# Other starting bytes for the token rows that TensorE streams in a hybrid decoder layer

## The chip, the cores and the metric

The kernel runs on one core of a Trainium2 chip. The metric is the device time of one execution in microseconds (us). Before the change it is 1539.64 us, the median of 3 runs (1539.16 to 1542.01). The execution that the profiler recorded took 1543.23 us; its span, from the first to the last instruction, is 1541.5 us.

## The reference

One layer of a decoder trunk: 4096 new tokens and 64 sample tokens, model width 1024. What matters here is the first of its steps, the projection of all 4160 tokens through one weight matrix of 1024 by 2816:

```python
h = _rmsnorm(x, g_pre)
z = h @ w_in
cb, cc, ch, cg, q, k, v, ag, mq, mg = _split_cols(z)
...
y = jnp.concatenate([out_a, out_b, out_c], axis=-1) @ w_out
return x + _rmsnorm(y, g_post), new_conv, new_k, new_v
```

Between the two products stand a gated short convolution, a sliding window attention with sinks, and a cross attention into 256 memory tokens. All of it is float32.

## The kernel before, in words

The kernel has two parts. The first, up to about 935 us, is the input projection; the second is the attention and the output projection (line 1501).

**How a float32 product is made.** TensorE is fed float32r operands. To keep float32 accuracy each operand is split into a rounded part `hi` and a remainder `lo`, and a product is three matmuls: weights hi times tokens hi, weights hi times tokens lo, weights lo times tokens hi. `product` (lines 370 to 376) does that for four slices of 128 contraction rows: 12 matmuls of 128x128 weights by 260 token columns into one PSUM bank. Line 375 is the matmul, with its weight load.

**How the projection is staged.** `w_in` has 22 column tiles of 128. They are done in three phases of 4, 4 and 3 pairs of tiles (`PHASES`, line 44). The tokens go in 8 blocks of 520, each two halves of 260 columns. A block with a pair of column tiles is a 2x2 by 2x2 block product with Strassen's scheme in Winograd's form, seven products instead of eight (`PRODUCTS`, line 41). Only the first two blocks of the first phase take the plain eight (`PLAIN_BLOCKS`, line 45, `plain_block`, line 676). So a step is one of the seven token operands (B11, B21, T2, T3, T1, B22, T4) used by the 4 or 3 pairs ("quads" in the code, loop at line 983): 48 matmuls of line 375 in the first two phases, 36 in the third. All in all there are 7488 of them: 2 blocks x 8 products x 4 x 12 = 768 plain ones, then 6 x 7 x 4 x 12 = 2016, 8 x 7 x 4 x 12 = 2688 and 8 x 7 x 3 x 12 = 2016.

**What sets the order.** The order of all engines' instructions in the projection is written out by hand (`tc.manual_schedule`, line 699). In each step the next step's token operand is split first (`h_split(i + 1)`, line 946): ScalarE casts x to `hi` (line 365) and VectorE subtracts to `lo` (line 366). Each instruction handles 128 x 1040 elements, four rows of 260 per partition. `x_split` (line 584) does the same row by row in the plain blocks. VectorE and ScalarE also add the finished banks into the z tiles (`evict`, line 378).

**Where the operands lie.** `hi` and `lo` come from the pool `hp`, two buffers each. A buffer holds per partition four rows of `XR` = 320 elements, 1280 bytes, of which 260 are used; `split_tile` (lines 357 to 361) says at which element the 260 begin, from the list `begins` (line 355), whose two entries are taken in turn, so that each of the two buffers keeps one of them. 1280 is five times 256, and the buffers begin at multiples of 256 bytes, so all four rows of a buffer have the same starting byte modulo 256. Before, these are:

| buffer pair | hi rows begin at, modulo 256 | lo rows begin at, modulo 256 |
|---|---|---|
| A | 32 | 160 |
| B | 64 | 192 |

Steps alternate between A and B. The weight slices of the first three quads (w_0, w_1, w_2 in the profile's names, pool `wa`) begin at 0 modulo 256, those of the fourth (w_3, pool `wb`, `w_slot` at line 173) at 224; a slice of 128 columns is 512 bytes.

Of the kernel before, what the change touches and what calls it, by code (L numbers as in the profile page):

```python
# [52 lines left out]
def hybrid_layer(ctx: ExitStack, tc: tile.TileContext, a: dict):  # L53
# [298 lines left out]
                tc.keep_in_program_order(ins)  # L352
            store(hd[b][o], ops[o])

    begins = {"hi": [8, 16], "lo": [40, 48]}

    def split_tile(tag, name):

# [1333 lines left out]
```

## Time and profile before

| what | value |
|---|---|
| median of 3 runs | 1539.64 us (1539.16 to 1542.01) |
| profiled execution | 1543.23 us, span 1541.5 us |
| granted TensorE clock, mean | 0.998 |
| input projection, line 375 | about 6 to 935 us |
| attention and output projection | about 935 to 1541 us |

Names such as `hi_5T` or `w_0S` are the program's tile names with buffer numbers left out: `hi_5T` is the rounded part of one of block 5's T operands, `w_0S` the weights of quad 0 for one of the S operands. PE is TensorE's matmuls, PEld its weight loads, DVE VectorE, ACT ScalarE, POOL GpSimd. A matmul's recorded duration runs past the start of the next one, since matmuls are pipelined; what a matmul costs is the distance from its start to the next start. In the chain of waits, "x36" after a piece says that 36 instructions in a row were on the chain.

### The profile page before, as it was taken

The numbers are of one execution on the slowest core, as the hardware profiler recorded it, in microseconds if no ns is written. First come the engines' busy times: TensorE is split into PE (matmuls) and PEld (weight loads), VectorE is DVE, ScalarE is ACT, GpSimd is POOL, SyncE is SP. The second block draws the span as 40 slices with busy tenths as digits, with TensorE's granted clock in tenths as the row PEclk, the third lists the DMA queues.
The fourth block names the chain that finished last, engine by engine and source line by source line (L and its number), as shares of the span: only waits on it lengthen the run. The fifth ranks groups of instructions, "written<-read, shape, count | busy, mean of one in ns | idle before, by whom it ended". The sixth has DMA issues, their size and how long they took to land.

```text
span 1541.5 us, 30150 instructions
## 1 busy us (share of the span) xinstructions
PE 1529.6 (99%) x11331; PEld 1407.2 (91%) x11331; DVE 1147.0 (74%) x2055; ACT 806.8 (52%) x2039; POOL 380.8 (25%) x604
## 2 busy tenths in 40 slices
PE   9999999999999999999999999999999999999998
PEld 9999999999999999999999998788888888888877
DVE  6779888898988777887787678766666666666643
ACT  6776566476222222354454447665566556555632
POOL 0223332211400000000101203544444444444310
PEclk9999999999999999999999999999999999999999
DMA  9989999778755333678777789976767676776433
GB/s 267 195 215 242 268 281 268 272 240 290 193 180 180 126 125 126 216 221 286 232 264 229 227 293 257 225 161 155 158 148 148 148 155 157 155 159 152 130 109 96
DMA packets 177942, 306.28 MB, mean 199 GB/s; under 512 B 33925, under 2 KB 107653, under 8 KB 177765
## 3 DMA queue, kind: packets, MB, share of 16 engines
q1 hardware_dynamic: 130901, 227.38, 47.5%
q0 software_dynamic: 46176, 75.92, 24.0%
q8 instruction: 90, 1.47, 0.4%
q10 hardware_dynamic: 720, 1.05, 0.2%
q14 instruction: 55, 0.45, 0.1%
HBM read 197.23 MB, written 108.05 MB: 198 GB/s over the span
## 4 chain that ended last, share of the span: by engine, by line
PE 93%; DVE 3%; DMA 2%; issue 1%; ACT 0%; POOL 0%; DVEq 0%; SPq 0%; POOLq 0%; ACTq 0%
PE c L375 55%; PE y L1501 22%; PE ws L1255 4%; PE wo L1097 2%; PE wt L1278 2%; PE xs L1191 2%; PE xt L1206 2%; PE wo L1227 2%; PE wo L1233 1%; PE mem_acc L798 1%; DMA qd<-z 1%; DVE z L382 0%; DMA wr_1A<-in_w_in 0%; DMA xr<-in_x_p 0%; DVE wo L186 0%
## 5 line engine op out<-in xcount | busy, mean ns | idle before, releaser
L1501 PE MATMUL y<-wo,mh 128*128 128x512 f32 (+1 forms) x1040 | 350.8, 400 | 0.0
L382 DVE TENSOR_TENSOR z<-c,z 128x520 f32<-128x520 f32 (+1 forms) x308 | 194.5, 644 | 94.3 <-PE c L375 92.5
L1501 PEld LDWEIGHTS y<-wo,mh 128*128 128x128 f32 x1040 | 194.5, 188 | 39.3 <-issue 2.4
L1501 PE MATMUL y<-wo,ml 128*128 128x512 f32 (+1 forms) x520 | 201.8, 388 | 0.0
L1268 ACT ACTIVATE sm<-sm,wnm 128x128 f32<-128x128 f32 x256 | 99.6, 391 | 60.8 <-DVE wnm L1262 59.3
L1200 POOL TENSOR_SCALAR xp<-xp,xrd 128x256 f32<-128x256 f32 x128 | 74.9, 593 | 209.2 <-DVE xrd L1196 209.2
L1501 PEld LDWEIGHTS y<-wo,ml 128*128 128x128 f32 x520 | 98.2, 189 | 16.5
L1192 DVE TENSOR_REDUCE xmx<-xs 128x2 f32<-128x512 f32 x64 | 44.1, 689 | 59.7 <-PE xs L1191 59.6
L1280 ACT COPY wpt<-wt 128x512 f32<-128x512 f32 x64 | 37.3, 583 | 88.9 <-PE wt L1278 86.4
L1255 PEld LDWEIGHTS ws<-kst,q 128*128 128x128 f32 x512 | 70.3, 191 | 5.6 <-ACT xp L1195 0.7
L1508 DVE TENSOR_TENSOR yn<-y,gpost 128x512 f32<-128x512 f32 (+1 forms) x66 | 45.0, 682 | 39.9 <-PE y L1501 39.6
L1255 PE MATMUL ws<-kst,q 128*128 128x256 f32 x512 | 73.7, 284 | 0.4 <-ACT xp L1195 0.4
L1509 ACT ACTIVATE y<-y 128x512 f32<-128x512 f32 (+1 forms) x66 | 38.6, 585 | 64.1 <-DVE yn L1508 64.1
L746 POOL CAST wmask<-negs 128x256 uint8<-128x256 f32 x1 | 1.0, 1037 | 267.2 <-DMA negs<-in_wmask 267.2
L1288 POOL TENSOR_SCALAR_AFFINE_SELECT wpt<-wpt 128x512 f32<-128x512 f32 x64 | 52.8, 825 | 42.2 <-ACT wpt L1280 39.2
L1195 ACT ACTIVATE xp<-xs,xnm 128x256 f32<-128x256 f32 x128 | 59.0, 465 | 7.1 <-DVE xnm L1193 7.1
L1130 POOL DMA_DIRECT2D q<-qd x64 | 42.9, 675 | 70.7 <-DVE wo L186 60.9
L1519 DVE SCALAR_TENSOR_TENSOR xr<-yn,yst,xr 128x1024 f32<-128x1024 f32 (+2 forms) x34 | 43.5, 1281 | 15.5 <-POOL yst L1515 13.4
L1119 POOL DMA_DIRECT2D kst<-qd x64 | 38.7, 617 | 63.8 <-PE xt L1206 41.5
L1258 DVE COPY_PREDICATED sm<-wmask,ws 128x256 f32<-128x256 uint8 x124 | 52.1, 436 | 2.5 <-ACT sm L1257 2.3
L1285 POOL TENSOR_SCALAR_AFFINE_SELECT wpv<-wpt 128x512 f32<-128x512 f32 x62 | 40.4, 652 | 52.1 <-ACT wpt L1280 52.0
L384 ACT COPY z<-c 128x520 f32<-128x520 f32 (+1 forms) x44 | 24.4, 554 | 52.9 <-PE c L375 50.0
(962 smaller groups left out, 5121.4 us busy)
## 6 DMA issues: line engine op xcount, KB each, us to landing
q<-qd POOLq DMA_DIRECT2D x64, 384.0 KB, 7.2
xr<-in_x_p SPq DMA_DIRECT2D x32, 512.0 KB
nat<-in_x_p SPq DMA_DIRECT2D x39, 416.0 KB
o_yp<-xr SPq DMA_DIRECT2D x31, 512.0 KB
md<-th POOLq DMA_DIRECT2D x48, 260.0 KB, 6.3
qd<-zh SPq DMA_DIRECT2D x48, 260.0 KB
qd<-z SPq DMA_DIRECT2D x48, 260.0 KB
kst<-qd POOLq DMA_DIRECT2D x60, 192.0 KB, 5.9
```

Of the source, the lines that this page charges most:

```text
L375: TE.matmul(bank[:, :HW], l, r, start=first and i == 0, stop=last and i == 3 * KH - 1)
L382: add = lambda dst, other: V.tensor_tensor(dst, c, other, op=ALU.add)
L1192: V.tensor_reduce(mx[:, :nb], s, axis=AX.X, op=ALU.max)
L1195: S.activation(p[:, i, :], s[:, i, :], AF.Exp, bias=nm[:, i : i + 1], scale=SCALE, accum_out=den[:, i : i + 1])
L1200: G.tensor_scalar(p[:, i, :], p[:, i, :], rd[:, i : i + 1], 0.5, op0=ALU.mult, op1=ALU.mult)
L1255: TE.matmul(s3[:, hh, :], self.q[:, 4 + 2 * (2 * half + hh) + kvh, i * P : i * P + P], self.kst[:, 2 * kvh + part, i * P : i * P + 2 * P], ...
L1258: V.copy_predicated(sm[:, 2 * half : 2 * half + 2, :], third["wmask"], third["negs"] if first else s3[:, :, 0:P])
L1268: S.activation(sm[:, hh, :], sm[:, hh, :], AF.Exp, bias=nm[:, hh : hh + 1], scale=SCALE, accum_out=den[:, hh : hh + 1])
L1288: G.affine_select(p3, p3, pattern=[[0, 4], [1, P]], compare_op=ALU.is_ge, fill=0.0, base=0, channel_multiplier=-1)
L1501: TE.matmul(acc, self.hl[l][:, k], wo[k][c0 // 512][:, r, c0 % 512 : c0 % 512 + c1 - c0], start=j == 0, stop=j == passes * KT - 1)
L1508: V.tensor_tensor(yn[:m, c0:c1], acc[:m], gpost[:m, c0:c1], op=ALU.mult)
L1519: V.scalar_tensor_tensor(self.xr[:m, cs], yn[:m, cs], st[:m, 3:4], self.xr[:m, cs], op0=ALU.mult, op1=ALU.add)
```

## The change

One line: the elements at which the 260 columns of a row begin. The rows of `hi` begin at 16 or 144 bytes modulo 256, those of `lo` at 80 or 208. In 16-byte units these are the odd numbers 1, 9, 5 and 13, where before they were the even ones 2, 4, 10 and 12. The weights stay at 0 and 224, which are even numbers of 16 bytes.

```diff
-    begins = {"hi": [8, 16], "lo": [40, 48]}
+    begins = {"hi": [4, 36], "lo": [20, 52]}
```

Tile sizes, addresses of buffers, instructions and their order stay as they are. The last row of a buffer now ends at element 52 + 260 = 312 of 320.

## Prediction

> **What bounds the kernel now.** I read the page first, then the chain of waits in order of time, then the timeline of two steps of the projection, then the stretches.
>
> ```profile
> span 1541.5 us, 30150 instructions
> PE 1529.6 (99%) x11331; PEld 1407.2 (91%) x11331; DVE 1147.0 (74%) x2055; ACT 806.8 (52%) x2039; POOL 380.8 (25%) x604
> ...
> PE 93%; DVE 3%; DMA 2%; issue 1%; ACT 0%; POOL 0%; DVEq 0%; SPq 0%; POOLq 0%; ACTq 0%
> PE c L375 55%; PE y L1501 22%; PE ws L1255 4%; PE wo L1097 2%; PE wt L1278 2%; PE xs L1191 2%; PE xt L1206 2%; PE wo L1227 2%; PE wo L1233 1%; PE mem_acc L798 1%; DMA qd<-z 1%; DVE z L382 0%; DMA wr_1A<-in_w_in 0%; DMA xr<-in_x_p 0%; DVE wo L186 0%
> ```
>
> TensorE is the chain for 93% of the span, and 55 points of that are line 375, the only line whose operands the change moves. The chain in order of time gives its pieces (start, length, count):
>
> ```profile
> 113.80 238.98 PE c L375 x1992
> 355.91 305.13 PE c L375 x2542
> ...
> 786.70 0.95 PE ws L1255 x8
> 787.65 4.24 PE c L375 x36
> 791.89 0.96 PE ws L1255 x8
> 792.85 4.32 PE c L375 x36
> ...
> 797.62 4.24 PE c L375 x36
> ...
> 802.30 4.33 PE c L375 x36
> ...
> 1007.23 2.78 PE y L1501 x12
> ```
>
> Two things are to be seen. In the first two phases matmuls follow one another without a wait: 238.98 / 1992 = 119.97 ns and 305.13 / 2542 = 120.04 ns. In the third, whole steps of 36 alternate between 4.32 to 4.33 us (120 ns each) and 4.24 us (117.8 ns each). Same shape, same count, same weight pool: only the buffer pair, so the starting bytes, and the moment differ. So the cost of a matmul does depend on something like the edited line.
>
> The timeline shows the same inside a step of 48. Here are the starts of the four quads of a step on pair A (240.36), of the next on pair B (246.10), and of the one after.
>
> ```profile
> 240.36 0.28 PE L375 MATMUL c<-hi_5T,w_0S 128*128 128x260 f32 x1
> ...
> 241.80 0.28 PE L375 MATMUL c<-hi_5T,w_1S 128*128 128x260 f32 x1
> ...
> 243.24 0.28 PE L375 MATMUL c<-hi_5T,w_2S 128*128 128x260 f32 x1
> ...
> 244.68 0.28 PE L375 MATMUL c<-hi_5T,w_3S 128*128 128x260 f32 x1
> ...
> 246.10 0.28 PE L375 MATMUL c<-hi_5T,w_0S 128*128 128x260 f32 x1
> ...
> 247.53 0.28 PE L375 MATMUL c<-hi_5T,w_1S 128*128 128x260 f32 x1
> ...
> 248.97 0.28 PE L375 MATMUL c<-hi_5T,w_2S 128*128 128x260 f32 x1
> ...
> 250.41 0.28 PE L375 MATMUL c<-hi_5T,w_3S 128*128 128x260 f32 x1
> ...
> 251.25 0.29 PE L375 MATMUL c<-lo_5T,w_3S 128*128 128x260 f32 x1
> 251.38 0.41 PE L375 MATMUL c<-hi_5T,w_3S 128*128 128x260 f32 x2
> ...
> 251.87 0.28 PE L375 MATMUL c<-hi_5B,w_0S 128*128 128x260 f32 x1
> ```
>
> Twelve matmuls of a quad take 1.44, 1.44, 1.44 and 1.42 us on pair A, and 1.43, 1.44, 1.44 and 1.46 us on pair B. The fourth quad has its weights at 224 instead of 0 modulo 256: with them pair A is cheaper (118.3 ns) and pair B dearer (121.7 ns). With the weights at 0 both pairs cost 120 ns here, though pair B costs 117.8 in the third phase. So a price depends on rows and weights together, and one pair of addresses can have two.
>
> What meets there is visible in the weight loads of the same stretch:
>
> ```profile
> 240.12 0.19 PEld L375 LDWEIGHTS c<-hi_5T,w_3S 128*128 128x128 f32 x1
> 240.24 0.19 PEld L375 LDWEIGHTS c<-hi_5T,w_0S 128*128 128x128 f32 x1
> 240.36 0.19 PEld L375 LDWEIGHTS c<-lo_5T,w_0S 128*128 128x128 f32 x1
> ```
>
> Every matmul has its own load, and the load for the next starts when the matmul starts (both 240.36): while 260 columns stream, 128 columns of weights are read from the same memory.
>
> **The change, part by part.** It adds and removes no instruction, no wait and no transfer, and moves none past a queue. Three kinds of instruction touch the moved rows.
>
> The matmuls of line 375: 7488 by the loops, 2 x 8 x 48 plain, then 6 x 7 x 48, 8 x 7 x 48 and 8 x 7 x 36. All lie on the path (the pieces above hold no wait), so 1 ns each is 7.5 us. No row shows float32r rows at an odd multiple of 16 bytes, so I bound the price. Cheapest of the rows: 4.24 / 36 = 117.8 ns. Dearest: 1.46 / 12 = 121.7 ns over a quad, and one spacing of 0.13 us between two starts (251.25 to 251.38) inside it. A floor below that comes from other shapes. Eight matmuls of 256 columns take 0.95 us, 119 ns each; twelve of 512 take 2.78 us, 231.7 ns each. So a column costs (231.7 - 119) / 256 = 0.44 ns, 260 of them 114.5 ns, and about 5.5 ns is there whatever the width (an estimate from these rows); that is what could go if it is a collision of the two reads and the new places remove it.
>
> I take 120 ns, no change. It is the price that three of four quads pay now on both pairs, although the pairs stand differently to the weights: 32 and 160 against 64 and 192. A price that stayed when rows moved by 32 bytes is the likeliest after a move by 16. The fourth quad pays 118.3 and 121.7, on average 120 again. Term: 7488 x 0 = 0 us.
>
> [...]
>
> The two splits, ScalarE's cast to `hi` and VectorE's subtraction to `lo`, write rows that begin elsewhere (and VectorE reads `hi` there):
>
> ```profile
> L365 ACT CAST hi_5T<-x_5T 128x1040 fp32r<-128x1040 f32 x8 | 8.5, 1066 | 13.4 <-PE c L375 9.7 <-issue 3.7
> L366 DVE TENSOR_TENSOR lo_5T<-x_5T,hi_5T 128x1040 fp32r<-128x1040 f32 x8 | 9.9, 1239 | 1.2 <-ACT hi_5T L365 1.2
> ...
>   DVE lo_0B L366: 0.8, 2
>   DVE lo_0T L366: 0.5, 2
>   DVE lo_2T L366: 0.5, 2
> ```
>
> The last three rows are of line 375's own waits: with all 7488 matmuls, TensorE waited for `lo` 1.8 us. A split takes 1.07 + 1.24 = 2.3 us and is made one step ahead, in a step of 5.74 us, so 3.4 us of cover hide even a doubling of it; a cheaper split gives at most those 1.8 us. Bound on this term: -1.8 to about +2 us, taken as 0. Without that cover each nanosecond of the pair would count once in each of some 160 steps. Between these, other engines have little room to matter:
>
> ```profile
> 50.00:340.00 290.00, 289.89 (x2412) 289.44 (x2411) 242.90 (x312) 185.41 (x334) 77.90 (x125) 1.00 0.92 250
> 340.00:550.00 210.00, 209.84 (x1750) 209.44 (x1749) 176.75 (x241) 76.20 (x107) 24.68 (x28) 1.00 0.57 185
> ```
>
> The columns are length, then busy time of PE, PEld, DVE, ACT and POOL, granted clock, share of the DMA engines, GB/s. In the first phase the DMA engines are 92% busy and VectorE 84%: up to some 8% of TensorE's time could go before they become the bound. No case below asks for more than 5%.
>
> The sum: the profiled execution has 1541.5 us of span and 1.7 us around it (1543.23 in all); 0 + 0 leaves that. The runs shown have a median of 1539.64, 3.6 us below the profiled one, so I forecast 1539.6 us in the terms of the median. A measurement of this kernel can tell about 0.2%, 3.1 us, from no change; that is 0.41 ns of a matmul.
>
> **The rivals.**
>
> *The cheap price everywhere.* Pair B's third-phase steps show that a regular stream at 117.8 ns exists with the weights at 0. If the new places lead to it from any moment, the plain blocks and first two phases (5472 matmuls) save 120.0 - 117.8 = 2.2 ns each, 12.0 us, and half of the third phase's 56 steps save 0.09 us each, 2.5 us: 1541.5 falls by 14.5, the median to 1525. For it: rows and weights now all begin at even multiples of 16 bytes, so an odd start separates them in a way not seen yet. Against it: pair B reaches that price in the third phase and not in the second with the same addresses, so the moment decides as well.
>
> *The collision goes.* If the 5.5 ns are gone, 7488 x 5.5 = 41 us, 1498. TensorE's time falls under 5%, which the 92% of the DMA engines still allow. For it: the constant is there. Against it: it is there at all shapes and places that the rows show, none of which comes below 117.8.
>
> *The dear price everywhere (slower).* On pair B with weights at 224 the quads run at 121.7 ns. If rows at an odd multiple of 16 bytes meet the weights as badly, with weights at 0 too, it is (121.7 - 120) x 7488 = 13 us: 1552. It decides from the point at which a quad of twelve with w_0 passes 1.445 us (120.4 ns). For it: such a quad exists in each step on pair B. Against it: it is one place out of four.
>
> *Worse than any quad seen.* If each matmul took the single spacing of 0.13 us, rounded; its neighbours being 0.12, I put it at 125 ns: 5 x 7488 = 37 us, 1577. Against it: no twelve in a row do so.
>
> **How the numbers follow.** No change 0.31, the cheap price 0.28, no collision 0.09, the dear price 0.25, worse 0.07. I rank no change first since the same 120 ns holds on two different pairs, but not by much: the fourth quad shows that moves of this size shift a price by 2 ns either way. Faster by over 0.2%: 0.28 + 0.09 = 0.37; within 0.2%: 0.31; slower: 0.25 + 0.07 = 0.32. The forecast's own range is 1536.5 to 1542.7. The range for 8 times in 10 takes in the cheap and the dear price with the splits' bounds and some of what lies beyond: 1518 to 1556; left out are most of 0.09 and 0.07.
>
> **What would show it.** The piece of 1992 matmuls in the chain: 239 us if I am right, 234.6 at the cheap price, 242.4 at the dear one, 228 without collision. The quads of a step in the timeline: 1.44 us, against 1.41, 1.46 and 1.37. The third phase's steps of 36: still a mixture of 4.24 and 4.33 us if moment and place decide together; one length alone if the place decides. The cast and the subtraction should stay at 1.07 and 1.24 us, and lines 1501 and 1255 at their prices, since their operands lie elsewhere. I am wrong if the spacing of matmuls with w_0 leaves 120 ns by more than 0.4, or if line 375 starts to wait for `hi` or `lo`.

## The result and the profile after

The change makes the kernel slower by a third of a per cent.

| | median | lowest to highest | profiled execution | its span |
|---|---|---|---|---|
| before | 1540.07 us | 1539.06 to 1542.01 | 1543.23 us | 1541.5 us |
| after | 1545.24 us | 1544.15 to 1548.24 | 1547.25 us | 1545.5 us |

The ratio of the times is 1.0035, with a 95% interval of 1.0024 to 1.0046: 5.2 us, between 3.7 and 7.1. All engines carry out the same instructions in the same order. The page after begins:

```profile
span 1545.5 us, 30150 instructions
...
PE 1533.0 (99%) x11331; PEld 1410.5 (91%) x11331; DVE 1146.0 (74%) x2055; ACT 806.6 (52%) x2039; POOL 380.5 (25%) x604
```

The busy time of TensorE's matmuls rose by 3.4 us, that of its weight loads by 3.3, and no other engine's rose. The chain of waits in order of time (start, length, count) has the pieces that were 238.98 us for 1992 matmuls, 305.13 us for 2542, and 4.24 or 4.33 us for a step of the third phase:

```profile
114.30 240.66 PE c L375 x1992
...
486.50 205.67 PE c L375 x1703
...
788.06 4.34 PE c L375 x36
...
793.35 4.32 PE c L375 x36
...
798.62 4.32 PE c L375 x36
...
803.38 4.33 PE c L375 x36
```

240.66 / 1992 and 205.67 / 1703 are both 120.8 ns, where it was 120.0. In the third phase the steps of 4.24 us are gone: those without a wait now take 4.31 to 4.36 us, about 120 to 121 ns a matmul, on both buffer pairs.

The timeline shows one step on pair A (hi at 16, lo at 80) and the next on pair B (144, 208). The starts of their quads are:

```profile
241.66 0.29 PE L375 MATMUL c<-hi_5T,w_0S 128*128 128x260 f32 x1
...
243.12 0.28 PE L375 MATMUL c<-hi_5T,w_1S 128*128 128x260 f32 x1
...
244.57 0.28 PE L375 MATMUL c<-hi_5T,w_2S 128*128 128x260 f32 x1
...
246.02 0.28 PE L375 MATMUL c<-hi_5T,w_3S 128*128 128x260 f32 x1
...
247.49 0.28 PE L375 MATMUL c<-hi_5T,w_0S 128*128 128x260 f32 x1
...
253.25 0.29 PE L375 MATMUL c<-hi_5B,w_0S 128*128 128x260 f32 x1
```

Pair A's quads take 1.46, 1.45, 1.45 and 1.47 us, its step 5.83 us or 121.5 ns a matmul; pair B's step takes 253.25 - 247.49 = 5.76 us, 120.0 ns. Before, the two steps took 5.74 and 5.77 us. Only pair A became dearer in this stretch.

Pair A doesn't pay that price all the time. TensorE waits for `lo` just before 358.1 us (0.15 us) and again just before 444.8 us (0.21 us), and between these two waits pair A's steps take as long as pair B's. Here are the starts of one of them and of the step behind it:

```profile
392.52 0.28 PE L375 MATMUL c<-hi_1B,w_0A 128*128 128x260 f32 x1
...
398.29 0.28 PE L375 MATMUL c<-hi_1T,w_0S 128*128 128x260 f32 x1
```

That is 5.77 us, 120 ns a matmul. For some 230 us before the first of these waits and again after the second, pair A's steps take 5.83 us, 121.4 ns, with the same starting bytes. So even within the first two phases the moment takes part: each of these changes came with a wait.

From here on "spacing" is the mean distance between the starts of one matmul of line 375 and the next, over the whole trace, with the distances of 150 ns and more (waits) left out. It was 119.73 ns and is 120.40 ns, and it rose in each phase: from 119.87 to 120.49, from 119.81 to 120.48 and from 119.41 to 120.17 ns. The mean difference, 0.68 ns before rounding, times 7488 is 5.1 us: nearly all of the measured 5.2 us.

Two smaller things changed. Line 375's own waits for `lo`, 1.8 us before, are now these:

```profile
  DVE lo_3T L366: 1.9, 2
...
  DVE lo_2T L366: 0.9, 3
...
  DVE lo_0T L366: 0.5, 2
  DVE lo_0B L366: 0.3, 1
```

That is 3.6 us, 1.8 more. (The view counts the idle time of a weight load and of its matmul one by one, so a wait stands in it twice.) And the last matmul of line 375 starts 6.4 us later (941.07 us after the span's start, 934.69 before), 0.5 us of which the first already had. The span grew by 4.0 us only, so the second part of the kernel gave 2.4 us back, 1.4 of them in the first long wait of the chain there. In the chain before it is

```profile
942.87 10.70 DMA qd<-z
```

and in the chain after

```profile
949.17 9.35 DMA qd<-z
```

### The profile page after: what moved, and what is told of

It is laid out like the page before. It is cut to its first block, busy times and chain, and to the rows that moved or that the text cites. A ratio compares the mean times of both kernels' runs of the same rounds, so it can differ in the third digit from the quotient of the medians.

```text
span 1545.5 us, 30150 instructions
## 1 busy us (share of the span) xinstructions
PE 1533.0 (99%) x11331; PEld 1410.5 (91%) x11331; DVE 1146.0 (74%) x2055; ACT 806.6 (52%) x2039; POOL 380.5 (25%) x604
## 3 DMA queue, kind: packets, MB, share of 16 engines
q8 instruction: 90, 1.47, 0.4%
## 4 chain that ended last, share of the span: by engine, by line
PE 92%; DVE 4%; DMA 2%; issue 1%; ACT 1%; SPq 0%; POOL 0%; DVEq 0%; POOLq 0%; ACTq 0%
PE c L375 53%; PE y L1501 22%; PE ws L1255 4%; PE wo L1097 2%; PE wt L1278 2%; PE xs L1191 2%; PE xt L1206 2%; PE wo L1227 2%; PE wo L1233 1%; PE mem_acc L798 1%; DMA qd<-z 1%; DVE z L382 0%; DMA xr<-in_x_p 0%; DMA ws20A<-in_w_in 0%; DVE wo L186 0%
```

## The experiments

The theory is that the time goes with line 375's spacing and that the spacing is set by where the moved rows stand to the weights. The rivals: that odd multiples of 16 bytes are bad as such; that the place modulo 64 decides, or the distance between `hi` and `lo`; that only one of the two rows matters; and that the moment decides. All edits are given against the kernel after, but for half_before; ratios are to the kernel before, run beside it.

### Other places of the same rows: rows_0, rows_32, rows_48, odd_128

```diff
-    begins = {"hi": [4, 36], "lo": [20, 52]}
+    begins = {"hi": [0, 32], "lo": [16, 48]}     # rows_0
+    begins = {"hi": [8, 40], "lo": [24, 56]}     # rows_32
+    begins = {"hi": [12, 44], "lo": [28, 60]}    # rows_48
+    begins = {"hi": [4, 20], "lo": [36, 52]}     # odd_128
```

The first three move all rows of the change by the same 16 bytes or a multiple, so that hi and lo stay 64 bytes apart; odd_128 uses the change's own four bytes but pairs them 16 with 144 and 80 with 208.

rows_0: 

> All rows begin at 0 modulo 64 bytes (hi 0 and 128, lo 64 and 192 modulo 256), lo 64 bytes behind hi as in the changed kernel. Theory 'relative place' (a matmul's price is set by row start minus weight start modulo 64 bytes): differences 0 with w_0 to w_2 and 32 with w_3, so pair B's prices of the kernel before, 117.8 to 120 ns and 121.7 ns: 1531 to 1541 us. Theory 'odd start' (an odd multiple of 16 bytes is dear by itself, wherever the weights are): even, so as before, 1540 +- 2 us. Theory 'spacing' (it is the 64 bytes between hi and lo of a pair, which were 128 before): as the changed kernel, 1545 +- 2 us.

rows_32: 

> All rows begin at 32 modulo 64 bytes (hi 32 and 160, lo 96 and 224). Relative place: difference 32 with w_0 to w_2, 0 with w_3, so pair A's prices of the kernel before, 120 and 118.3 ns: 1536 to 1540 us. Odd start: even, 1540 +- 2 us. Spacing: 1545 +- 2 us.

rows_48: 

> All rows begin at 48 modulo 64 bytes (hi 48 and 176, lo 112 and 240), the other odd place. Relative place: the differences 16 and 48 change over from the changed kernel, so another time than its 1545 us, by over 2 us. Odd start: odd again, 1545 +- 2 us. Spacing: 1545 +- 2 us.

odd_128: 

> Rows at 16 modulo 64 bytes as in the changed kernel, but lo 128 bytes behind hi, as before (hi 16 and 80, lo 144 and 208). Relative place and odd start: as the changed kernel, 1545 +- 2 us. Spacing: as before, 1540 +- 2 us.

| kernel | hi / lo of A; of B (modulo 256) | median | ratio (95%) | spacing |
|---|---|---|---|---|
| after | 16 / 80; 144 / 208 | 1545.24 us | 1.0035 (1.0024 to 1.0046) | 120.40 ns |
| rows_0 | 0 / 64; 128 / 192 | 1537.30 us | 0.9989 (0.9979 to 0.9998) | 119.35 ns |
| rows_32 | 32 / 96; 160 / 224 | 1542.61 us | 1.0021 (1.0012 to 1.0030) | 120.27 ns |
| rows_48 | 48 / 112; 176 / 240 | 1541.45 us | 1.0013 (1.0005 to 1.0022) | 120.08 ns |
| odd_128 | 16 / 144; 80 / 208 | 1538.41 us | 0.9999 (0.9990 to 1.0007) | 119.58 ns |

Odd multiples of 16 bytes as such fall: odd_128 has only odd ones and is as fast as before, rows_32 has only even ones and is slower. The place modulo 64 falls too ("relative place" in the expectations), since odd_128 and the change have all rows at 16 modulo 64 and differ in ratio by 0.36%; nor did rows_32 come within the 1536 to 1540 us expected by it. And 64 bytes between hi and lo are not bad in themselves: rows_0 has them and is a little faster than before. The piece of 1992 in rows_0's chain, and five of its third-phase steps:

```profile
113.69 237.94 PE c L375 x1992
...
779.62 4.25 PE c L375 x36
...
784.82 4.39 PE c L375 x36
...
790.15 4.25 PE c L375 x36
...
794.84 4.39 PE c L375 x36
...
814.72 4.32 PE c L375 x36
```

The steps on pair A (0 / 64) cost 118.1 ns a matmul. Those on pair B (128 / 192) cost 121.9 ns at the dearest (4.39 us, 7 of the phase's 28) and 120.0 to 120.4 otherwise (4.32 us). The phase's means are 118.0 and 120.7 ns: with the weights at 0 in both, 128 bytes make 2.7 ns on average and nearly 4 at most. The other three have the piece of 1992 as follows. The chain of rows_32:

```profile
112.86 239.75 PE c L375 x1992
```

of rows_48:

```profile
114.01 239.03 PE c L375 x1992
```

and of odd_128:

```profile
113.06 238.59 PE c L375 x1992
```

The spacing's difference from before times 7488 gives -2.8, +4.0, +2.6 and -1.1 us in the order of the table; by the ratios it was -1.7, +3.2, +2.0 and -0.2. Spacing is what the time follows.

### Both buffers alike: pair_16_80, pair_144_208

```diff
-    begins = {"hi": [4, 36], "lo": [20, 52]}
+    begins = {"hi": [4, 4], "lo": [20, 20]}      # pair_16_80
+    begins = {"hi": [36, 36], "lo": [52, 52]}    # pair_144_208
```

pair_16_80: 

> The changed kernel with both buffer pairs at its pair A's places, hi 16 and lo 80 modulo 256. If the place decides the price, modulo 256: pair A's quads of the changed kernel, 120.7 ns with w_0 to w_2 and 121.7 with w_3, about 121 ns, 1549 us. If only the place modulo 128 counts, or mainly the moment: the same as the next run, within 2 us.

pair_144_208: 

> The changed kernel with both pairs at pair B's places, hi 144 and lo 208. If the place decides modulo 256: pair B's quads, 120.0 ns with all four weights, 1541 us. If only modulo 128: the same as the run before this one, within 2 us.

pair_16_80 took 1542.98 us, 1.0022 (1.0012 to 1.0032), spacing 120.33 ns; pair_144_208 took 1541.44 us, 1.0010 (1.0001 to 1.0020), spacing 120.10 ns. The piece of 1992 in the chain of pair_16_80:

```profile
113.78 240.12 PE c L375 x1992
```

and of pair_144_208:

```profile
113.15 239.60 PE c L375 x1992
```

Pair A's places are the dearer ones by 0.2 ns only, and the 1549 us expected for them didn't come: the two runs lie 1.5 us apart, within the 2 us by which "modulo 128, or mainly the moment" was to be told. The two alike don't come to the change's time either: their mean ratio is 1.0016, the change's is 1.0035. In pair_16_80 the quads with weights at 0 have 120.1 ns; in the kernel after, the same pair has 120.7. So the place of a pair doesn't fix its price. Whether the other pair's steps take part or the moment does, these two runs can't tell.

### Only one of the two rows moved: hi_only, lo_only

```diff
-    begins = {"hi": [4, 36], "lo": [20, 52]}
+    begins = {"hi": [4, 36], "lo": [40, 48]}     # hi_only
+    begins = {"hi": [8, 16], "lo": [20, 52]}     # lo_only
```

hi_only: 

> Only the hi rows moved (16 and 144), lo as before (160 and 192). Theory 'each row pays by itself': hi is read in two of three matmuls, so two thirds of the change, 1543.5 us, and this difference and that of the next run add up to 5 us. Theory 'in company' (a price belongs to the places of a hi row, its lo row and the weights together): the two differences need not add up; off by over 2 us, and either may even be below 1540.

lo_only: 

> Only the lo rows moved (80 and 208), hi as before (32 and 64). Each row pays by itself: one third of the change, 1541.7 us. In company: not additive, off by over 2 us.

hi_only took 1533.88 us, 0.9968 (0.9956 to 0.9981), spacing 119.02 ns; lo_only 1541.56 us, 1.0014 (1.0006 to 1.0023), spacing 120.04 ns. The piece of 1992 in the chain of hi_only:

```profile
112.80 237.43 PE c L375 x1992
```

and of lo_only:

```profile
112.78 239.47 PE c L375 x1992
```

The change's half that moves `hi` is a gain by itself, the half that moves `lo` a loss. Together they should give -0.32 + 0.14 = -0.18%, and give +0.35%. lo_only's time is the one that "each row pays by itself" gives (1541.7 us), but hi_only's is nearly 10 us below it (1543.5). So neither row has a price of its own: hi and lo count together. That the weights count too is shown further down.

### Shorter weight loads: half_before, half_after

```diff
-                TE.matmul(bank[:, :HW], l, r, start=first and i == 0, stop=last and i == 3 * KH - 1)
+                n = P if i % 3 == 0 or i == 3 * KH - 1 else 64
+                TE.matmul(bank[:n, :HW], l[:, :n], r, start=first and i == 0, stop=last and i == 3 * KH - 1)
```

Seven of the twelve matmuls of a quad load 64 weight columns instead of 128; half_before has this in the kernel before (`begins` as there), half_after in the kernel after.

half_before: 

> The kernel before, with 7 of every 12 matmuls of line 375 (all but the four hi by hi and the last) using only the first 64 of their 128 weight columns, so that half the correction terms of the other 64 output rows are left out. The rows stream as they did. Theory 'two reads' (the weight load beside the stream costs the time over a bare stream): a load half as long costs less, the mean spacing of line 375 falls from 119.7 ns by 2 to 4 ns, the time by 15 to 30 us. Rival 'rows alone' (the stream's own places cost it): spacing and time stay, 119.7 ns and 1540 +- 3 us.

half_after: 

> The same left out of the changed kernel. Two reads: falls as much, and the changed kernel's extra 5 us over the kernel before shrink to 0 to 3 us. Rows alone: 1545 +- 3 us, still 5 us above the one before.

half_before took 1535.48 us, 0.9971 (0.9960 to 0.9981), spacing 119.07 ns; half_after 1537.75 us, 0.9991 (0.9982 to 1.0000), spacing 119.41 ns. Weight loads of half_after in the timeline, one of each kind:

```profile
243.27 0.13 PEld L376 LDWEIGHTS c<-lo_5T,w_2S 128*64 128x64 f32 x1
243.38 0.19 PEld L376 LDWEIGHTS c<-hi_5T,w_2S 128*128 128x128 f32 x1
```

The load is shorter by nearly a third, the spacing by 0.66 ns before and by 1.0 ns after, less than the 2 to 4 ns expected of "two reads". "Rows alone" missed as well: half_before isn't within 3 us of 1540. What the change adds shrinks from 0.68 to 0.34 ns, and from 5 us to 2.3. That is the direction which "two reads" expected, and it is weak: shorter loads in 7 of 12 matmuls leave the spacing at 119 ns.

### A distance meant to be good: rows_0_64

rows_0's pair A at 0 / 64 had the cheapest quads with weights at 0, so both buffers got it.

```diff
-    begins = {"hi": [4, 36], "lo": [20, 52]}
+    begins = {"hi": [0, 0], "lo": [16, 16]}
```

> Both buffer pairs at hi 0 and lo 64, the cheaper pair of the run with rows at 0 modulo 64, where its quads took 118.1 ns (weights at 0) and 120.0 ns (weights at 224). If these prices go with the places: mean 118.5 ns, 1531 us. If the moment decides, or the other pair's steps prepared it: back at 119.3 to 120 ns, 1537 to 1541 us.

1530.25 us, 0.9946 (0.9932 to 0.9959), spacing 118.45 ns: faster than both kernels, by 0.54% than before, and as expected if the price goes with the places (1531 us). The chain:

```profile
113.07 236.68 PE c L375 x1992
...
775.80 4.24 PE c L375 x36
...
780.98 4.24 PE c L375 x36
...
786.17 4.24 PE c L375 x36
```

and the quads of a step in the timeline:

```profile
244.00 0.28 PE L375 MATMUL c<-hi_5T,w_0S 128*128 128x260 f32 x1
...
245.42 0.28 PE L375 MATMUL c<-hi_5T,w_1S 128*128 128x260 f32 x1
...
246.84 0.28 PE L375 MATMUL c<-hi_5T,w_2S 128*128 128x260 f32 x1
...
248.25 0.28 PE L375 MATMUL c<-hi_5T,w_3S 128*128 128x260 f32 x1
...
249.69 0.28 PE L375 MATMUL c<-hi_5B,w_0S 128*128 128x260 f32 x1
```

1.42, 1.42, 1.41 and 1.44 us: the three quads with weights at 0 pay 118 ns, in each phase and on both buffers, the one with weights at 224 pays 120.

### The fourth quad's weights: rows_0_64_w128, rows_0_64_w0

```diff
+    wb_stack.enter_context(tc.tile_pool(name="shift", bufs=1, side="right")).tile([P, 24], F32, name="shift")
```

With this unused tile ahead of pool `wb` and `begins` of rows_0_64, w_3 lies at 128 modulo 256 (rows_0_64_w128). For rows_0_64_w0 the tile has 56 elements, `place` (a tile of 2 * KH * HW + 32 elements) is made 32 elements shorter, and `begins` is hi [32, 32], lo [48, 48]: the rows lie at 0 / 64 again, and all weights at 0.

rows_0_64_w128: 

> The same, with the fourth quad's weights moved from 224 to 128 modulo 256 (a tile of 96 bytes before their pool). If places modulo 128 decide: all quads as with weights at 0, 117.7 to 118.1 ns, 1526 us. If modulo 256 counts: the fourth quad takes another price than the others and another than 120.0 ns. If the moment decides: 1537 to 1541 us.

rows_0_64_w0: 

> Rows at hi 0 and lo 64 in both pairs, and now all four quads' weights at 0 modulo 256. Theory 'in company, modulo 256': the fourth quad falls from 120.0 to the others' 117.9 to 118.1 ns, 7488/4 x 0.73 (its share) x 2 ns = 3 us below rows_0_64's 1530.3: 1527. Rival 'the fourth quad is dear by its turn' (it comes last in a step, or its tiles lie far off): it stays at 120 ns and the time at 1530.

rows_0_64_w128 took 1531.80 us, 0.9951 (0.9938 to 0.9963); rows_0_64_w0 took 1530.54 us, 0.9935 (0.9921 to 0.9948). The chain of rows_0_64_w128 has

```profile
113.36 236.24 PE c L376 x1992
```

and that of rows_0_64_w0

```profile
112.73 187.01 PE c L376 x1583
```

that is 118.6 and 118.1 ns a matmul, where rows_0_64 has 118.8. By quads, from the starts of all of them, those with w_3 cost 120.0 ns at 224, 120.1 at 128 and 117.8 at 0, and those with w_0 to w_2 117.9 to 118.1 in all three. So the fourth quad was not dear by its turn, and the place modulo 128 isn't enough: 128 and 0 have different prices. That 224 and 128 have the same one was not expected. The whole kernel's spacing with all weights at 0 is 117.86 ns, which should be worth 4.4 us against rows_0_64; by the ratios 1.7 us came (1527 us was expected), and the intervals overlap. In its trace the distances of 150 ns and more between two matmuls of the line (L376 there) add up to 14.9 us, 12.5 in rows_0_64, and among the line's waits are

```profile
  ACT w_0A L183: 2.5, 2
  DVE lo_2T L367: 2.4, 4
```

In rows_0_64 they were 1.3 and 0.7 us. So some 2 of the 4.4 us turned into waits for the engines that feed TensorE. Of the rest, 0.6 us is a later first matmul (6.49 against 5.87 us) and 0.6 a longer second part; the spans differ by the 1.1 us that is left.

### Place or distance: joint_32, weights_32

```diff
+    const.tile([P, 8], F32, name="pad")
-    begins = {"hi": [4, 36], "lo": [20, 52]}
+    begins = {"hi": [0, 0], "lo": [16, 16]}      # joint_32
+    begins = {"hi": [56, 56], "lo": [8, 8]}      # weights_32
```

The pad of 32 bytes moves every tile behind it. In both, w_0 to w_2 lie at 32 and w_3 at 224. In joint_32 the rows move along, to 32 / 96; in weights_32 they stay at 0 / 64.

joint_32: 

> Rows and the first three quads' weights moved together by 32 bytes: hi 32, lo 96, weights 32. Theory 'difference' (only the distance of the rows to each other and to the weights counts): quads with w_0 to w_2 keep rows_0_64's 118.1 ns. Theory 'absolute place': they take another price; rows at 32 and 96 with weights at 0 took 120.4 ns. The output projection's operands move by 32 bytes too, so the first 930 us are to be read, by line 375's pieces of the chain.

weights_32: 

> Rows at hi 0 and lo 64, only the first three quads' weights moved, from 0 to 32. Theory 'difference', and 'in company' at large: another price than 118.1 ns, by over 0.5 ns. Rival 'rows alone' (the rows' places set it, whatever the weights): still 118.1 ns.

joint_32 took 1535.32 us, 0.9976 (0.9965 to 0.9986), spacing 118.48 ns; weights_32 took 1548.78 us, 1.0059 (1.0045 to 1.0073), spacing 120.75 ns. The chain of joint_32:

```profile
113.11 236.74 PE c L376 x1992
...
783.88 4.25 PE c L376 x36
...
789.08 4.25 PE c L376 x36
```

and that of weights_32:

```profile
115.36 240.71 PE c L376 x1992
...
788.43 4.35 PE c L376 x36
...
793.73 4.35 PE c L376 x36
```

The third phase reads w_0 to w_2 only, and there joint_32 repeats rows_0_64's steps of 4.24 us, at 4.25 us, with rows and weights 32 bytes on. Over the whole trace these quads cost 117.9 ns (118.1 in rows_0_64), while rows at 32 / 96 with the weights left at 0 paid 120.4 ns (mean of pair A of rows_32, w_0 to w_2). weights_32 has rows_0_64's rows, and the steps of its third phase cost 4.34 or 4.35 us in the chain where they hold no wait; its quads with w_0 to w_2 cost 120.8 ns. So it is the distance of rows and weights that has the price here, not a place.

The fourth quads need care. In joint_32 w_3 did not move along, so its distance to the rows did change, and its quads went from 120.0 to 121.1 ns; that the piece of 1992 is as long as in rows_0_64 (236.68 us) comes from two differences that cancel. And in weights_32 the fourth quads have rows and weights where rows_0_64 has them, but cost 120.5 ns instead of 120.0: the distance is not quite all.

As a time joint_32 gained only 3.7 of the 9.4 us that its spacing gives. Against rows_0_64, at the same spacing, its last matmul of the line starts 3.0 us later, most of it waits, and the second part, whose tiles the pad moved as well, takes 2.2 us longer. So its spacing, not its time, is the evidence here. weights_32 has the same pad, so between these two only the rows differ: 2.27 ns x 7488 = 17.0 us by the spacing, 13.5 us by the medians.

## Why the prediction was wrong

**The step that failed** is "I take 120 ns, no change", with its reason, "a price that stayed when rows moved by 32 bytes is the likeliest after a move by 16". The term was 0 and measured +0.68 ns, 5.1 us. The two pairs that shared 120 ns looked like two samples of a price that doesn't depend on place. The runs show that it does: rows_0_64 and weights_32 have the same rows, weights that lie 32 bytes apart, and 118.1 against 120.8 ns with w_0 to w_2, and rows_0's two pairs, both with weights at 0, have means of 118.0 and 120.7 ns in the third phase. So the two pairs were two distances whose prices were alike, and said little about a third. The quoted rows held a warning: the fourth quads differed by distance, the 4.24 us steps were a second price of pair B, and "on average 120 again" assumed that a move keeps an average.

**The nearest rival was the slower one** (the dear price), whose condition, a quad with w_0 past 1.445 us, was met on pair A (1.45 to 1.46 us) and not on pair B (1.44). Its reason did not hold: odd multiples of 16 bytes are not dear as such, as odd_128 shows (0.9999), and in hi_only odd `hi` rows even gain (0.9968). Its size was 1.7 ns everywhere; 0.68 came. In the first two phases pair A's steps rose from 119.5 to 121.3 and 121.0 ns, pair B's stayed at 120; in the third, pair A stood at 120.4 (120.1 before) and pair B went from 118.7 to 119.9, since it lost its steps at some 118 ns. (Before, 11 of its 28 steps there paid 119.9 ns already: the alternation that the prediction read from the chain held for part of the phase.) The piece of 1992 told it: 240.66, between the 239 of no change and the 242.4 of the dear price. That the measured time lies in the range for 8 times in 10 is owed to the rivals that the range takes in, not to the forecast's reason.

**What was sound.** Nearly all of the change lies in line 375. The splits stayed at their price; the groups of the first 930 us after are

```profile
L365 ACT CAST hi_5T<-x_5T 128x1040 fp32r<-128x1040 f32 x8 | 8.5, 1064 | 13.3 <-PE c L375 9.5 <-issue 3.8
...
L366 DVE TENSOR_TENSOR lo_5T<-x_5T,hi_5T 128x1040 fp32r<-128x1040 f32 x8 | 9.9, 1239 | 1.6 <-ACT hi_5T L365 1.6
```

at 1.06 and 1.24 us, and the waits for `lo` grew by 1.8 us, inside the bound of 2, though that they would grow at all was named as a sign of being wrong. The other engines didn't become the bound: the DMA engines' share of the first stretch is 0.93 (0.92 before). The bounds of a matmul's price, 117.8 to 121.7 ns, hold every kernel's spacing (117.86 ns in rows_0_64_w0 to 120.75 ns in weights_32), though single groups of quads lie above (122.0 ns on pair A with w_3 in the first phase of the kernel after). The third phase was to show "one length alone if the place decides"; its steps now lie between 4.31 and 4.36 us, so the moment still takes part.

**What stays open.** That the two reads meet in the memory is the author's reading and was not shown: shorter loads took 0.66 and 1.0 ns off the spacing, a step of 32 bytes between rows and weights made 2.7 ns (rows_0_64, weights_32), and no run shows why. Nor does any show why one pair of distances has two prices (pair B before in two phases, pair A after on the two sides of a wait); the steps next to it or how the two streams stand to each other after a wait may decide, and were not told apart. What the some 118 ns below all of this consists of is open too: the shorter loads took 1 ns at most off it.

## What to carry to other kernels

Where each matmul has its own weight load and TensorE is the bound, as here (the chain for 93% of the span before), the starting bytes of the streamed rows against the weights are worth a sweep: an element offset in one line moved this kernel from 1.0035 to 0.9946 of its time. Read a price by buffer and by weight slice before calling it constant, and put the same distance in both buffers, since a good distance on one pair was lost in the mean here (rows_0, 118.0 and 120.7 ns in the third phase, 0.9989; rows_0_64, 0.9946). Rows that began at the weights' byte (hi) and 64 bytes on (lo) were the best here; treat that as a starting point, not a rule.

## What the runs showed of the hardware beside it

A 32-byte shift of the weights under the same rows moved the mean price of a matmul from 118.1 to 120.8 ns (rows_0_64, weights_32, quads with w_0 to w_2); single steps of 36 lay between 4.24 and 4.40 us (rows_0_64, rows_48), 118 to 122 ns, and the whole kernel's time spanned 1.2% (0.9935 to 1.0059). The same starting bytes had two prices: in the second phase of the kernel after, pair A went from one to the other (121.4 and 120.0 ns) at waits of TensorE, and in the third its steps went from 4.36 us (start 671.80) to 4.32 us (680.48) with no wait between. The effects of the places of hi and lo did not add up: moving hi gained 0.32%, moving lo lost 0.14%, moving both lost 0.35%. And a weight load of 64 columns took 0.13 us instead of 0.19, yet 7 such loads in 12 made the mean spacing only 0.66 to 1.0 ns shorter.
